# Making the first FFN column blocks' weight operands, and the sums of the values' weights, in other stages

## The chip, the cores and the metric

The kernel runs on one core of a Trainium2 chip (trn2). The metric is the device time of one execution in microseconds (us). The engines are TensorE (PE, its weight loads PEld), VectorE (DVE), ScalarE (ACT), GpSimd (POOL) and SyncE (SP). Each has a queue of its own that it works through in order; DMAs are issued from such a queue too.

## What is computed

Two layers on x of 1024 tokens by 1024 features, in float32. Layer 0 mixes the tokens with a chunked gMLP, layer 1 with differential attention, and each is followed by an FFN with a causal convolution of three taps. Each of the four parts stands between two RMSNorms and is added to its input:

```python
for layer in range(DEPTH):                       # 2
    y = rmsnorm(h, norm_g[layer, 0])
    y = gmlp_mixer(y, ...) if layer == 0 else diff_attention(y, ...)
    h = h + rmsnorm(y, norm_g[layer, 1])
    y = rmsnorm(h, norm_g[layer, 2])
    y = conv_ffn(y, w_up, conv_w, conv_b, w_down)   # 1024 -> 2 x 2816 -> 1024
    h = h + rmsnorm(y, norm_g[layer, 3])

def conv_ffn(x, w_up, conv_w, conv_b, w_down):
    h = causal_dwconv(x @ w_up, conv_w, conv_b)
    g, u = h[..., :D_FF], h[..., D_FF:]
    return (gelu(g) * u) @ w_down
```

## The kernel before

**Splits and passes.** Every float32 operand of a product is split (`split`, L170 and L173) in a hi part, which ScalarE casts to fp32r, and a lo part, the rest, which VectorE subtracts. A product takes three passes: hi by hi, hi by lo, lo by hi, all in `mm` (L162). Each 128x512 matmul of these is one instruction.

**Seven products for eight.** The FFN's up projection, its down projection and the values of the attention are computed as Strassen-Winograd products: the operands are cut in 2x2 blocks, sums of blocks are formed on both sides (S1 to S4 of the activations, T1 to T4 of the weights), and seven products take the place of eight. The sums of weights cost subtractions on POOL:

- the up projection forms them for each of its 22 column blocks in `winograd_weights` (L1044 and the lines behind it), from two raw loads of 512 KB, then splits seven parts;
- the down projection's sums are made beforehand by `weight_sum` (L438 to L447): two loads, four POOL subtractions of 128x256, two stores to DRAM (`td`). The values' weights `b_wv` go the same way into `tv`, in eight such sums: six in the loop of the mixer over the gate's column blocks g (at g = 4 to 7), two in layer 0's up projection (at j = 2 and 3). All loads and stores are issued from SP.

**The mixer** (`gmlp`) computes v in two halves, normalises it, mixes it with small matmuls in `gate` (L643 to L645: a copy on ScalarE, an addition on VectorE, an addition on POOL), and forms u in eight column blocks g (L693, L694, L677). At g = 4 `distances` makes the bias of the attention, 62 POOL operations (L596). Then the out projection begins, with operands `ops` split from the products.

**The FFN's opening** (`ffn`): column blocks 0 and 1 are begun together while the last rows of the normalised activations are still being turned (`xs`, L344, and transposes L334). Their weights are raw loads; their sums on POOL are partly pinned in program order (`early_sums`), their parts are split as they are needed.

**The down projection** (`down`) runs seven products of 11 blocks each, in the order A11·B11, A22·T4, A12·B21, A11·T2, A21·T1, A12·B22, A22·T3. Its operands are cast from `raw` into t8 tiles: one pair of blocks after the other, the last two pairs of a product ahead of the end, and for A22·T3 five pairs ahead, whose weights then lie in t8 tiles too. While A12·B22 and A22·T3 run, `end` normalises finished rows, and the transposes for the next stage follow.

**The values** (`values`) run the same kind of products behind layer 0's FFN, with T1 to T4 loaded from `tv` and S1 to S4 made by `finish`.

**What sets the order.** The program is traced in the order of the text, with `later` for work that is due after a number of matmul columns. A scheduler then orders each engine's instructions by when their inputs are expected; `keep_in_program_order` pins an instruction behind all that was traced before it on its engine. Tiles come from pools with a fixed number of buffers: t8 (8 KB of each partition, 15 buffers), wr (raw weights, 4), w4 (split weights, 7). A new tile waits until a buffer of its tag is free, and the buffers are handed out in program order.

Of the kernel before, what the change touches and what calls it, by code (L numbers as in the profile page):

```python
# [13 lines left out]
ALU = mybir.AluOpType  # L14
# [50 lines left out]
def trunk(ctx: ExitStack, tc: tile.TileContext, io):  # L65
# [202 lines left out]
    class WinogradOperand:  # L268
# [43 lines left out]
        def finish(self, tile=lambda: t8(F32R, (P, 4, 512))):  # L312
            for n in ("S2", "S1", "S4", "S3") if self.whole else ("S2", "S1", "S3", "S4"):
                hi, lo = self.part[n] = tile(), tile()
                for kt in range(4):
                    if self.whole and n == "S2":
                        self.sums((kt, slice(None)), nc.vector, nc.gpsimd)
                    split(hi[:, kt, :], lo[:, kt, :], self.raw[n][:, kt, :])
                yield
# [109 lines left out]
    def weight_sum(w, o, j):  # L429

        a = wpool.tile([P, 2, 2, 256], F32, tag="wr", name=nm("wr"), bufs=4)
        kt, cs = j // 2, slice(j % 2 * 256, j % 2 * 256 + 256)
        for k in range(2):
            src = w[kt + k * o.shape[1]].rearrange("p (b c) -> p b c", b=2)
            nc.sync.dma_start(a[:, k], src[:, :, cs])  # L438

        def rest():  # L440
            sub = nc.gpsimd.tensor_tensor
            sub(a[:, 0, 0], a[:, 0, 1], a[:, 0, 0], ALU.subtract)
            sub(a[:, 0, 1], a[:, 1, 1], a[:, 0, 1], ALU.subtract)
# [19 lines left out]
    def down(l, h_in, h_out, g_post, g_pre, y_next):  # L463
# [45 lines left out]
        def product(a, b, ahead=(), first=None, at=3, tail=SHORT_TAIL, wide=0):  # L509
# [11 lines left out]
            for m, (k, n) in enumerate(pairs[:-tail]):  # L521
                xw = ahead[m] if m < len(ahead) else operands(a, b, k, n)
                if m > 1 or b != "T4":
                    some(2)
                for i in range(4):
                    part(i, k, n, *xw)
                if m == at and first:
                    first()
            xws = [operands(a, b, k, n, m >= tail - wide) for m, (k, n) in enumerate(pairs[-tail:])]
# [10 lines left out]
        with tc.tile_pool(name=nm("out"), bufs=1) as pool:  # L540
# [40 lines left out]
    rd = dpool.tile([NT, P], F32, name="rd", tag="rd")  # L581

# [19 lines left out]
    def gmlp(y, y2, ahead):  # L602
        with tc.tile_pool(name="gm", bufs=1) as pool:
# [95 lines left out]
            for a in begun:  # L699
                a()  # L700
# [30 lines left out]
    def values(y):  # L731
# [7 lines left out]
        with tc.tile_pool(name="va", bufs=1) as pool:  # L739

            def product(a, b, groups=((0, 1), (2, 3))):
                ws = load(b)
# [25 lines left out]
            more = y.finish(lambda: pool.tile([P, 4, 512], F32R, tag="s", name=nm("s"), bufs=4))  # L768
            next(more)
            for t, r in product("A22", "T4"):  # L770
                nc.scalar.copy(v[:, t], r)
            next(more)
            for t, r in product("S2", "T2"):
                add(u2[:, t], r, u2[:, t], ALU.add)
                nc.gpsimd.tensor_tensor(v[:, t], v[:, t], u2[:, t], ALU.add)
            next(more)
            for t, r in product("S1", "T1"):
# [250 lines left out]

    def winograd_weights(pool, src, early):

        r1, r2 = raw_w(src[0], KT, P), raw_w(src[1], KT, P)
        b11, b21, b12, b22 = r1[:, 0:4, :], r1[:, 4:8, :], r2[:, 0:4, :], r2[:, 4:8, :]

        def part(b, pin=False):
            w = w4((2, 4, P))
            split(w[:, 0], w[:, 1], b, pin=pin)
# [7 lines left out]
        i = nc.gpsimd.tensor_tensor(t1, b12, b11, ALU.subtract)  # L1044
        if early:
            tc.keep_in_program_order(i)
        nc.gpsimd.tensor_tensor(t2, b22, t1, ALU.subtract)
        nc.gpsimd.tensor_tensor(t4, b21, t2, ALU.subtract)
        if early:
            yield  # L1050
            yield part(t4, True)
        nc.gpsimd.tensor_tensor(t3, b22, b12, ALU.subtract)
        for b in (t2, t1, t3, b22) if early else (t2, t1, t3, t4, b22):
            yield part(b)

    class Winograd:
# [47 lines left out]
        def early_sums(self):  # L1104
            next(self.weights)

# [35 lines left out]
    def ffn(l, y, h_in, h_out, g_pre, y2):  # L1142
        with tc.tile_pool(name=f"wg{l}", bufs=1) as wg, tc.tile_pool(name=f"ff{l}", bufs=1) as pool:
            def pair(j):
                return Winograd(wg, (io["ffn_up"][l, j], io["ffn_up"][l, NFF + j]), y, j < 2)
# [22 lines left out]
            for p in begun:  # L1168
                p.early_sums()
# [15 lines left out]
            for j in range(NFF):  # L1185
# [4 lines left out]
                if l == 0 and j in (2, 3):  # L1190
                    weight_sum(io["b_wv"], tv, KT - 4 + j)()
# [151 lines left out]
```

## Time and profile before

| | us |
|---|---|
| median of 3 runs | 2171.81 (2171.61 to 2175.49) |
| the profiled execution | 2170.53 |
| its span | 2168.8 |
| TensorE busy | 2113.0 (97%) |
| VectorE busy | 1660.5 (77%) |
| ScalarE busy | 1094.4 (50%) |
| POOL busy | 748.1 (34%) |

The profile is of one execution, whose own time stands beside the span. A timeline row gives the start, the duration (of several like instructions together, with their count behind x), the engine, the line, the operation, out<-in with shapes, and in brackets how long the engine was idle ahead of it and what ended that. The granted clock is the mean share of full speed at which TensorE ran in a stretch. The mean granted clock of the whole span is 0.995.

### The profile page before, as it was taken

The numbers are of one execution on the slowest core, as the hardware profiler recorded it, in microseconds if no ns is written. First come the engines' busy times: TensorE is split into PE (matmuls) and PEld (weight loads), VectorE is DVE, ScalarE is ACT, GpSimd is POOL, SyncE is SP. The second block draws the span as 40 slices with busy tenths as digits, with TensorE's granted clock in tenths as the row PEclk, the third lists the DMA queues.
The fourth block names the chain that finished last, engine by engine and source line by source line (L and its number), as shares of the span: only waits on it lengthen the run. The fifth ranks groups of instructions, "written<-read, shape, count | busy, mean of one in ns | idle before, by whom it ended". The sixth has DMA issues, their size and how long they took to land.

```text
span 2168.8 us, 27265 instructions
## 1 busy us (share of the span) xinstructions
PE 2113.0 (97%) x10008; PEld 1721.4 (79%) x10008; DVE 1660.5 (77%) x2031; ACT 1094.4 (50%) x1923; POOL 748.1 (34%) x691
## 2 busy tenths in 40 slices
PE   8989998999999999999999999999899999999998
PEld 7868776888888878887777777778688888888886
DVE  5755569878888786688588888866988888888756
ACT  7423435454545544465366665754555554454533
POOL 0463136666667000042001101222555666620012
PEclk9999999999999999999999999999999999999999
DMA  8332422544444562453411110233234444457324
GB/s 320 102 122 83 176 87 82 192 149 153 146 165 146 198 251 95 136 180 106 158 45 45 50 49 21 88 136 126 70 121 167 159 156 157 154 182 266 105 92 167
DMA packets 159270, 292.82 MB, mean 135 GB/s; under 512 B 12704, under 2 KB 77088, under 8 KB 159136
## 3 DMA queue, kind: packets, MB, share of 16 engines
q1 hardware_dynamic: 159136, 291.08, 39.3%
q8 instruction: 78, 1.28, 0.2%
q14 instruction: 56, 0.46, 0.1%
HBM read 214.49 MB, written 76.55 MB: 134 GB/s over the span
## 4 chain that ended last, share of the span: by engine, by line
PE 74%; DVE 9%; ACT 3%; issue 1%; POOL 0%; DMA 0%; DVEq 0%; ACTq 0%; POOLq 0%; SPq 0%
PE ps L162 70%; PE pst L162 2%; DVE t L173 2%; DVE w L173 1%; ACT e L885 1%; DVE t L1155 1%; PE pst L904 1%; PE pst L334 1%; DVE cols L1090 1%; DVE xs L344 0%; DVE e L891 0%; DVE h L385 0%; DVE sm L882 0%; DVE t L495 0%; ACT y L340 0%
## 5 line engine op out<-in xcount | busy, mean ns | idle before, releaser
L162 PE MATMUL ps<-t,w 128*128 128x512 f32 x4848 | 1150.8, 394 | 19.5 <-ACT tm L1086 7.8
L162 PEld LDWEIGHTS ps<-t,w 128*128 128x128 f32 x4848 | 899.2, 188 | 220.8 <-ACT tm L1086 11.6
L162 PE MATMUL ps<-w,t 128*128 128x512 f32 x2512 | 590.5, 392 | 9.0 <-ACT w L170 7.3
L162 PEld LDWEIGHTS ps<-w,t 128*128 128x128 f32 x2512 | 469.4, 188 | 107.1 <-ACT w L170 8.0
L173 DVE TENSOR_TENSOR w<-wr,w 128x512 fp32r<-128x512 f32 (+1 forms) x274 | 290.4, 1066 | 170.0 <-ACT w L170 84.3
L170 ACT CAST w<-wr 128x512 fp32r<-128x512 f32 (+1 forms) x276 | 219.1, 802 | 207.3 <-PE ps L162 195.2
L1155 DVE SCALAR_TENSOR_TENSOR t<-cols,cw,t 128x1023 f32<-128x1023 f32 (+1 forms) x176 | 264.1, 1500 | 18.9 <-ACT t L1153 16.8
L173 DVE TENSOR_TENSOR w<-wt,w 128x512 fp32r<-128x512 f32 x176 | 174.9, 1005 | 15.4 <-ACT w L170 15.2
L1086 ACT COPY tm<-ps 128x512 f32<-128x512 f32 x136 | 78.9, 580 | 146.7 <-PE ps L162 146.6
L173 DVE TENSOR_TENSOR t<-t,t 128x1024 fp32r<-128x1024 f32 (+1 forms) x124 | 134.0, 1109 | 14.4 <-ACT t L170 14.0
L170 ACT CAST t<-t 128x1024 fp32r<-128x1024 f32 (+1 forms) x124 | 105.7, 889 | 71.7 <-PE ps L162 59.4
L1153 ACT ACTIVATE t<-cols,cw 128x1024 f32<-128x1024 f32 x88 | 109.7, 1247 | 60.0 <-DVE cols L1090 59.8
L1044 POOL TENSOR_TENSOR wt<-wr,wr 128x512 f32<-128x512 f32 x44 | 67.3, 1529 | 195.5 <-DMA wr<-in_ffn_up 135.4
L162 PE MATMUL ps<-t,t 64*128 64x512 f32 (+4 forms) x792 | 128.3, 373 | 0.8 <-ACT e L885 0.4
L170 ACT CAST w<-wt 128x512 fp32r<-128x512 f32 x176 | 107.5, 622 | 23.2 <-PE ps L162 14.1
L559 POOL TENSOR_TENSOR v<-v,u 128x512 f32<-128x512 f32 x8 | 12.0, 1499 | 307.0 <-DVE u L558 307.0
L162 PEld LDWEIGHTS ps<-t,t 64*128 64x128 f32 (+1 forms) x792 | 90.3, 185 | 34.3 <-issue 11.0
L885 ACT ACTIVATE e<-ps,sm 128x128 f32<-128x128 f32 (+7 forms) x128 | 94.2, 744 | 28.8 <-DVE sm L877 22.7
L380 POOL TENSOR_SCALAR sm<-sm 128x1 f32<-128x1 f32 x32 | 22.3, 697 | 244.9 <-ACT y L378 244.6
L202 POOL TENSOR_SCALAR sm<-sm 128x1 f32<-128x1 f32 (+1 forms) x42 | 12.7, 303 | 263.7 <-ACT ot L924 161.2
L1090 DVE TENSOR_TENSOR cols<-ps,tm 128x512 f32<-128x512 f32 x132 | 90.1, 682 | 16.7 <-PE ps L162 15.0
L173 POOL TENSOR_TENSOR t<-wr,t 128x1024 fp32r<-128x1024 f32 (+1 forms) x16 | 36.4, 2282 | 167.9 <-ACT t L170 159.7
(156 smaller groups left out, 2480.4 us busy)
## 6 DMA issues: line engine op xcount, KB each, us to landing
wr<-in_ffn_up SPq DMA_DIRECT2D x88, 512.0 KB, 4.0
wr<-in_ffn_down SPq DMA_DIRECT2D x94, 256.0 KB, 3.7
pd<-t SPq DMA_DIRECT2D x88, 256.0 KB, 2.6
td<-wr SPq DMA_DIRECT2D x88, 256.0 KB, 2.5
wr<-td SPq DMA_DIRECT2D x40, 512.0 KB, 3.7
t<-pd SPq DMA_DIRECT2D x16, 1024.0 KB, 8.2
wr<-in_ffn_down SPq DMA_DIRECT2D x30, 512.0 KB, 3.6
hd<-h SPq DMA_DIRECT2D x24, 512.0 KB, 2.6
```

Source lines behind the costliest of these rows:

```text
L162: nc.tensor.matmul(o, a, b, start=first, stop=last, skip_group_check=onto)
L170: i = nc.scalar.copy(hi, src)
L173: return (engine or nc.vector).tensor_tensor(lo, src, hi.bitcast(F32), ALU.subtract)
L334: nc.tensor.transpose(pt[:, k * P:(k + 1) * P], xs[:, f:f + P], ident)
L380: nc.gpsimd.tensor_scalar(ss, sq[:, 0:1], sq[:, 1:2], EPS, ALU.add, ALU.add)
L885: nc.scalar.activation(e[:, :L], si[i], AF.Exp, bias=negm[:, i:i + 1], accum_out=sm[:, i:i + 1])
L904: nc.tensor.transpose(pt[:, k * P:(k + 1) * P], attn[:, c:c + P], ident)
L1044: i = nc.gpsimd.tensor_tensor(t1, b12, b11, ALU.subtract)
L1086: nc.scalar.copy(t, o)
L1090: nc.vector.tensor_tensor(o, a, b, ALU.add)
L1153: nc.scalar.activation(tt, src, AF.Identity, bias=c[:, 3:4], scale=c[:, 2:3])
L1155: nc.vector.scalar_tensor_tensor(tt[:, tap:], src[:, :S - tap], c[:, 2 - tap:3 - tap], tt[:, tap:], ALU.mult, ALU.add)
```

## The change

A new generator `presplit(l)` makes the split weight operands of the up projection's first two column blocks ahead of time and stores them to a DRAM buffer `ud[l]`. Each block takes two raw loads from SP into a t8 tile, four POOL subtractions, seven splits into t8 tiles and seven stores of 512 KB, issued from POOL's queue. `presplit(0)` is stepped through in the mixer's loop from g = 4 on, three steps at each half, and finished behind the loop; `presplit(1)` in layer 0's down projection, three steps behind each of the first four pairs of A12·B22 and the rest ahead of A22·T3.

The openings of both FFNs then load the seven parts of each block from `ud` into w4 buffers with SP, with no raw load, no sum and no split.

All eight sums of `b_wv` move into the product A21·T1 of layer 0's down projection, two behind each of its first four pairs. There they use a t8 tile in place of a wr tile, their first subtraction is pinned in program order, and their two stores are issued from POOL's queue.

In the values, T4, T2 and T1 are loaded and split ahead of the S parts that `finish` splits, and the casts of the S parts are pinned in program order.

```diff
-    def weight_sum(w, o, j):
+    def weight_sum(w, o, j, pin=False):
-        a = wpool.tile([P, 2, 2, 256], F32, tag="wr", name=nm("wr"), bufs=4)
+        if pin:
+            a = t8(F32, (P, 2, 2, 2, 256))[:, 0]
+        else:
+            a = wpool.tile([P, 2, 2, 256], F32, tag="wr", name=nm("wr"), bufs=4)
...
-            sub(a[:, 0, 0], a[:, 0, 1], a[:, 0, 0], ALU.subtract)
+            i = sub(a[:, 0, 0], a[:, 0, 1], a[:, 0, 0], ALU.subtract)
+            if pin:
+                tc.keep_in_program_order(i)
...
-                nc.sync.dma_start(o[k, kt][:, :, cs], a[:, k])
+                (nc.gpsimd if pin else nc.sync).dma_start(o[k, kt][:, :, cs], a[:, k])
...
+            beside = [lambda i=i: weight_sum(io["b_wv"], tv, i, True)() for i in range(KT if l == 0 else 0)]
             u4 = t8(F32, (P, 4, 512))
-            for i, r in product("A21", "T1"):
+            for i, r in product("A21", "T1", beside=[lambda n=n: (beside[2 * n](), beside[2 * n + 1]()) for n in range(len(beside) // 2)]):
...
-            for i, r in product("A12", "B22"):
+            early = presplit(1) if l == 0 else iter(())
+            def steps(n):
+                for _ in range(n):
+                    next(early, None)
+            for i, r in product("A12", "B22", beside=[lambda: steps(3)] * 4):
...
+            for _ in early:
+                pass
             for i, r in product("A22", "T3", tail=TAIL, wide=WIDE):
...
-            sums = {4: (0,), 5: (1, 2), 6: (3, 4), 7: (5,)}
-            begun = []
+            early = presplit(0)
             for g in range(8):
                 w = load_w(io["a_wu"][g], KT, P)
-                for a in begun:
-                    a()
-                begun = [weight_sum(io["b_wv"], tv, i) for i in sums.get(g, ())]
                 if g == 4:
                     distances()
                 for half in range(2):
+                    if g > 3:
+                        for _ in range(3):
+                            next(early, None)
...
+            t4 = load("T4")
             next(more)
-            for t, r in product("A22", "T4"):
+            for t, r in product("A22", "T4", ws=t4):
...
+    def presplit(l):
+        for p in range(2):
+            r = t8(F32)
+            for i in range(2):
+                nc.sync.dma_start(r[:, i, :].rearrange("p (k c) -> p k c", k=KT), io["ffn_up"][l, p + i * NFF])
+            b11, b21, b12, b22 = (r[:, i, h:h + 512].rearrange("p (k c) -> p k c", k=4) for i in (0, 1) for h in (0, 512))
+            yield
+            out = []
+            def put(n, b):
+                if not out:
+                    w = t8(F32R, (P, 2, 2, 4, P))
+                    out.extend((w[:, 0], w[:, 1]))
+                w = out.pop(0)
+                split(w[:, 0], w[:, 1], b)
+                nc.gpsimd.dma_start(ud[l][p, n], w.bitcast(F32))
+            for n, b in ((0, b11), (1, b21), (6, b22)):
+                put(n, b)
+                yield
+            for n, o, x, y in ((4, b11, b12, b11), (5, b12, b22, b12), (3, b22, b22, b11), (2, b21, b21, b22)):
+                nc.gpsimd.tensor_tensor(o, x, y, ALU.subtract)
+                yield
+                put(n, o)
...
     def winograd_weights(pool, src, early):
+        if early:
+            for n in range(7):
+                w = w4((2, 4, P))
+                nc.sync.dma_start(w.bitcast(F32), src[n])
+                yield w
+            return
...
-                if l == 0 and j in (2, 3):
-                    weight_sum(io["b_wv"], tv, KT - 4 + j)()
```

## Rows read from the trace of the kernel before

**Rows 1.** The page: the span, and the engines' busy times

```profile
span 2168.8 us, 27265 instructions
PE 2113.0 (97%) x10008; PEld 1721.4 (79%) x10008; DVE 1660.5 (77%) x2031; ACT 1094.4 (50%) x1923; POOL 748.1 (34%) x691
```

**Rows 2.** Busy time by stretch: span, PE, PEld, DVE, ACT, POOL, clock, DMA

```profile
122.00:160.00 38.00, 28.83 (x129) 23.50 (x128) 20.00 (x30) 10.44 (x19) 22.39 (x26) 0.87 0.41 132
...
171.00:215.00 44.00, 44.00 (x196) 36.44 (x196) 20.54 (x37) 12.71 (x18) 18.02 (x67) 1.00 0.19 62
```

**Rows 3.** Timeline of TensorE in the mixer: start, duration, line, operation, idle before

```profile
135.71 3.46 PE L162 MATMUL ps<-wsp,vp 128*128 128x128 f32 x15 [0.88 <-DVE vp L173]
140.97 13.20 PE L162 MATMUL ps<-t,w 128*128 128x512 f32 x48 [1.80 <-DVE t L644]
...
156.51 1.95 PE L162 MATMUL ps<-wsp,vp 128*128 128x128 f32 x15 [1.58 <-DVE vp L173]
```

**Rows 4.** Timeline of TensorE in layer 0's down projection

```profile
844.81 85.62 PE L162 MATMUL ps<-w,t 128*128 128x512 f32 x377
930.27 6.29 PE L162 MATMUL ps<-t,t 128*128 128x512 f32 x27
```

**Rows 5.** Timeline of POOL in the mixer

```profile
138.56 0.72 POOL L442 TENSOR_TENSOR wr<-wr 128x256 f32<-128x256 f32 x1 [5.51 <-DMA wr<-in_b_wv]
139.24 0.72 POOL L645 TENSOR_TENSOR t<-t,gt 128x256 f32<-128x256 f32 x1
```

**Rows 6.** Timeline of ScalarE in the mixer

```profile
139.99 0.37 ACT L643 COPY gt<-ps 128x256 f32<-128x256 f32 x1 [5.60 <-POOL t L645]
...
186.75 0.37 ACT L643 COPY gt<-ps 128x256 f32<-128x256 f32 x1 [12.52 <-POOL t L645]
```

**Rows 7.** Busy time by stretch, as rows 2, in the two openings

```profile
320.00:350.00 30.00, 23.78 (x100) 17.56 (x101) 29.09 (x37) 19.32 (x35) 19.32 (x12) 1.00 0.18 56
...
1528.00:1558.00 30.00, 23.71 (x100) 17.55 (x101) 29.09 (x35) 19.32 (x35) 18.85 (x12) 1.00 0.17 56
```

**Rows 8.** TensorE's waits from 310 to 375 us: total, times, longest

```profile
PE ps L162 <- ACT tm L1086: 3.9, 2, 2.1
PE ps L162 <- DVE w L173: 3.2, 3, 1.5
PE pst L334 <- DVE xs L344: 1.2, 1, 1.2
PE ps L162 <- ACT w L170: 0.9, 1, 0.9
```

**Rows 9.** The values: timelines of TensorE and VectorE, busy time by stretch

```profile
1005.99 4.39 PE L162 MATMUL ps<-w,s 128*128 128x512 f32 x12 [3.80 <-DVE w L173]
...
1004.72 3.48 DVE L173 TENSOR_TENSOR w<-wr,w 128x1024 fp32r<-128x1024 f32 x3
...
985.00:1050.00 65.00, 61.20 (x263) 49.94 (x262) 49.87 (x62) 21.21 (x32) 13.33 (x8) 0.97 0.34 115
```

**Rows 10.** VectorE's groups from 310 to 375 us: busy time, mean ns

```profile
L173 DVE TENSOR_TENSOR w<-wt,w 128x512 fp32r<-128x512 f32 x13 | 11.2, 876 | 0.0
L173 DVE TENSOR_TENSOR w<-wr,w 128x512 fp32r<-128x512 f32 x7 | 6.2, 914 | 0.0
```

**Rows 11.** Timelines of POOL and ScalarE in layer 0's down projection

```profile
867.10 2.14 POOL L559 TENSOR_TENSOR v<-v,u 128x512 f32<-128x512 f32 x1 [1.83 <-DVE u L558]
...
887.91 6.31 ACT L170 CAST t<-t 128x1024 fp32r<-128x1024 f32 x7
```

**Rows 12.** Instructions of two lines: shortest, median, longest ns, first and last start

```profile
L442 POOL TENSOR_TENSOR wr<-wr x52: 723/1182/1762, 102.0 to 1905.9; 128x256 f32<-128x256 f32 x52
...
L447 SPq DMA_DIRECT2D tv<-wr x16: 553/562/570, 104.5 to 375.2; - x16
```

**Rows 13.** Busy time by stretch, as rows 2, in layer 0's down projection

```profile
845.00:865.00 20.00, 20.00 (x90) 16.53 (x90) 12.49 (x13) 7.79 (x10) 3.59 (x3) 1.00 0.24 79
865.00:888.00 23.00, 23.00 (x103) 19.06 (x102) 7.46 (x7) 5.30 (x7) 2.40 (x2) 1.00 0.32 103
888.00:905.00 17.00, 17.00 (x77) 14.08 (x76) 14.62 (x16) 10.26 (x13) 0.00 (x0) 1.00 0.34 108
905.00:925.00 20.00, 20.00 (x90) 16.57 (x89) 16.68 (x18) 13.15 (x19) 3.22 (x4) 1.00 0.62 207
```

More of the change, by code (lines that the diff above doesn't have):

```diff
@@ L317, in finish @@
                         self.sums((kt, slice(None)), nc.vector, nc.gpsimd)
-                    split(hi[:, kt, :], lo[:, kt, :], self.raw[n][:, kt, :])
+                    split(hi[:, kt, :], lo[:, kt, :], self.raw[n][:, kt, :], pin=self.whole)
                 yield
@@ L507, in operands, with product @@
             return x, w
-        def product(a, b, ahead=(), first=None, at=3, tail=SHORT_TAIL, wide=0):
+        def product(a, b, ahead=(), first=None, at=3, tail=SHORT_TAIL, wide=0, beside=()):
             out = [bank1() for _ in range(4)]
@@ L528, in product @@
                     first()
+                if m < len(beside):
+                    beside[m]()
             xws = [operands(a, b, k, n, m >= tail - wide) for m, (k, n) in enumerate(pairs[-tail:])]
@@ L581, in trunk @@
     rd = dpool.tile([NT, P], F32, name="rd", tag="rd")
+    ud = [dpool.tile([2, 7, P, 2, 4, P], F32, name=f"ud{i}", tag=f"ud{i}") for i in range(2)]
     def distances():
@@ L698, in gmlp @@
                         weigh(g, half, u)
-            for a in begun:
-                a()
+            for _ in early:
+                pass
             flush()
@@ L739, in values, with product @@
         with tc.tile_pool(name="va", bufs=1) as pool:
-            def product(a, b, groups=((0, 1), (2, 3))):
-                ws = load(b)
+            def product(a, b, groups=((0, 1), (2, 3)), ws=None):
+                ws = ws or load(b)
                 os = [bank1() for _ in range(4)]
@@ L768, in values @@
             more = y.finish(lambda: pool.tile([P, 4, 512], F32R, tag="s", name=nm("s"), bufs=4))
+            t4 = load("T4")
             next(more)
-            for t, r in product("A22", "T4"):
+            for t, r in product("A22", "T4", ws=t4):
                 nc.scalar.copy(v[:, t], r)
+            t2 = load("T2")
             next(more)
-            for t, r in product("S2", "T2"):
+            for t, r in product("S2", "T2", ws=t2):
                 add(u2[:, t], r, u2[:, t], ALU.add)
                 nc.gpsimd.tensor_tensor(v[:, t], v[:, t], u2[:, t], ALU.add)
+            t1 = load("T1")
             next(more)
-            for t, r in product("S1", "T1"):
+            for t, r in product("S1", "T1", ws=t1):
                 add(u4[:, t], r, u2[:, t], ALU.add)
@@ L1027, in attention, with part @@
             return out
-    def winograd_weights(pool, src, early):
+    def presplit(l):
[20 more added lines that the diff above has]
+                put(n, o)
+    def winograd_weights(pool, src, early):
+        if early:
[4 more added lines that the diff above has]
+            return
         r1, r2 = raw_w(src[0], KT, P), raw_w(src[1], KT, P)
         b11, b21, b12, b22 = r1[:, 0:4, :], r1[:, 4:8, :], r2[:, 0:4, :], r2[:, 4:8, :]
-        def part(b, pin=False):
+        def part(b):
             w = w4((2, 4, P))
-            split(w[:, 0], w[:, 1], b, pin=pin)
+            split(w[:, 0], w[:, 1], b)
             return w
@@ L1043, in winograd_weights @@
         )
-        i = nc.gpsimd.tensor_tensor(t1, b12, b11, ALU.subtract)
-        if early:
-            tc.keep_in_program_order(i)
+        nc.gpsimd.tensor_tensor(t1, b12, b11, ALU.subtract)
         nc.gpsimd.tensor_tensor(t2, b22, t1, ALU.subtract)
         nc.gpsimd.tensor_tensor(t4, b21, t2, ALU.subtract)
-        if early:
-            yield
-            yield part(t4, True)
         nc.gpsimd.tensor_tensor(t3, b22, b12, ALU.subtract)
-        for b in (t2, t1, t3, b22) if early else (t2, t1, t3, t4, b22):
+        for b in (t2, t1, t3, t4, b22):
             yield part(b)
@@ L1102, in second @@
             self.add(self.cols[0][:, :512], self.product(self.first[1], "A12"), self.p1)
-        def early_sums(self):
-            next(self.weights)
         def early_part(self):
@@ L1144, in pair @@
             def pair(j):
-                return Winograd(wg, (io["ffn_up"][l, j], io["ffn_up"][l, NFF + j]), y, j < 2)
+                early = j < 2
+                src = [ud[l][j, n] for n in range(7)] if early else (io["ffn_up"][l, j], io["ffn_up"][l, NFF + j])
+                return Winograd(wg, src, y, early)
             def convolve(j, cols):
@@ L1167, in ffn @@
             begun = [pair(0), pair(1)]
-            for p in begun:
-                p.early_sums()
             cw = pool.tile([P, 2 * NFF, 4], F32, tag="cw", name="cw")
```

## The prediction

> **What bounds the kernel now.** The page's first section gives TensorE 2113.0 of 2168.8 us [rows 1]: nothing can be won beyond its 55.8 us of idle time and the few stretches in which its matmuls run slower. I therefore read the waits of TensorE first, then the busy times of the stretches that hold its gaps, then the timelines of the engines named there. The reader should see three places that the change touches, and one that it loads.
>
> *The mixer's end.* From 122 to 160 us TensorE is busy 28.83 of 38.00 us, so 9.2 us are gaps; the granted clock there is 0.87, about a quarter of the stretch at the lower of its two levels, 1.2 in place of 2.4 GHz [rows 2]. The gaps come ahead of small matmuls of the gate or right behind them, and the slower clock shows beside them: 15 matmuls of 128x128 take 3.46 us at 135.71 and 1.95 at 156.51, and 48 of 128x512 take 13.20 us at 140.97 [rows 3], where 48 times 0.227 us (377 in 85.62 us [rows 4]) are 10.9. That is 1.5 + 2.3, so 3.8 us of slowness; 13.0 us in all. The cause stands on POOL: the subtraction of a weight sum waited 5.51 us for its load, and the gate's addition L645 came only behind it [rows 5]; ScalarE waited 5.60 us for that addition before its copy L643 [rows 6], and the casts of the next tile stand behind that copy.
>
> *The two openings of the FFN.* From 320 to 350 us TensorE has 23.78 of 30.00, and 23.71 in the same stretch of layer 1, with VectorE at 29.09 of 30.00 in both [rows 7]. It waits for the lo parts of the weights, for the copies tm, and 1.2 us for xs [rows 8].
>
> *The values.* One gap of 3.80 us at 1005.99, for a lo part of T2 that VectorE began at 1004.72, behind splits of the S parts; the clock of 985 to 1050 is 0.97 [rows 9].
>
> *Layer 0's down projection*, where most of the new work goes, has no gap: 377 matmuls run from 844.81 to 930.43 without one [rows 4].
>
> **The change part by part.**
>
> *Weight sums out of the mixer.* Six of the eight leave POOL's queue in the mixer. With them goes the wait for its load [rows 5] and what follows from it. Bounds: 13.0 us if every gap and all the slow clock go, 4 if only the gaps right behind the 5.51 us wait do (0.88, 1.80 and the 1.5 of slowness at 135.71 [rows 3]). The waits are one cascade, so I take 11.
>
> *presplit(0) into the mixer.* Fourteen casts, 14 subtractions, 8 POOL subtractions, 4 loads and 14 stores, from the fifth of the eight column blocks on. There TensorE is full, 44.00 of 44.00, while VectorE has 20.54 and ScalarE 12.71 [rows 2]: 14 splits of 0.88 us on VectorE (the mean of w<-wt [rows 10]) are 12.3 us and fit. POOL is held by the distances, for which ScalarE waits 12.52 us without harm [rows 6]. The 15 buffers of tag t8 are almost all taken there, and the operands of the out projection queue for them behind presplit's tiles: 0 if presplit ends before 205 us, 6 if it ends at 215. I take 2.
>
> *The openings.* Of 20 weight splits on VectorE between 310 and 375 us [rows 10], 14 belong to the first two blocks and go; so do the 8 POOL subtractions beside them. Fourteen times 0.88 is 12.3 us of VectorE, more than the 6.2 us of gap in 320 to 350; VectorE would stand near 19 of 30. The gaps are 6.2 + 1.2 us in layer 0 and 6.3 + 1.2 in layer 1, 14.9 together; I leave 1 us in each for what is late next (the copies tm, or the first of the 512 KB loads that now wait for a w4 buffer), and take 13. The lower bound is 8: only the waits on w (3.2 and 0.9 a layer [rows 8]) go.
>
> *The values.* T4, T2 and T1 are split ahead of the S parts. VectorE's work is the same, only its order changes; the gap can go to the next S part. Bounds 0 and 5.2 (3.8, and 263 matmuls at 0.97 clock, some 1.4); I take 3.
>
> *What layer 0's down projection gets.* Eight weight sums in the product A21·T1 (32 POOL subtractions, 16 loads, 16 stores), presplit(1) in A12·B22 (8 POOL subtractions, 14 casts and splits, 14 stores). The first subtraction of each sum is pinned behind what POOL was given before, the last addition of v, which ends at 869.2 [rows 11]. A subtraction of this shape takes 0.72 to 1.76 us, median 1.18 [rows 12]; where VectorE is at 7.46 of 23 [rows 13] I take 0.8, later 1.2. No store has been issued from POOL in this trace. SP takes 0.56 us for one [rows 12], and this is the nearest row and my lower bound; the upper one is the longest of POOL's own instructions in the row beside it, 1.76. The value taken is 0.8, between the two and nearer to the row of a store. By that the sums end at 869.2 + 8 x (4 x 0.8 + 2 x 0.8) = 907.6. Behind them presplit(1)'s first block needs 4 subtractions and has 6 stores ahead of its last part: 4 x 1.2 + 6 x 0.8 = 9.6, so 917.2.
>
> Who waits: the operand tiles of A12·B22 and then of A22·T3 take their t8 buffers in program order behind presplit's, and their casts stand behind its casts on ScalarE; before, seven of them run in one burst at 887.91, far ahead of use [rows 11]. A22·T3's tail begins at 930.27 [rows 4], its first pair of 24 matmuls 5.45 us earlier, at 924.8; A12·B22 has 132 matmuls, 30.0 us, so it begins at 894.8 and needs its fourth pair at 911.2. That pair's cast (6.31 / 7 = 0.9 us [rows 11]) and split (3.48 / 3 = 1.2 [rows 9]) can follow the last presplit part's cast, 917.2 + 1.0 + 2.1: 920.3, so 9.1 us late. The second block ends one store, four subtractions and six stores later, 10.4 us; the operands of T3 come behind it with two casts and two splits a pair, while TensorE has been delayed by the 9.1 already, and I add 1 us. VectorE carries 14 more splits, 12.3 us, over 888 to 925, where it has 31.3 of 37 [rows 13]; what does not fit is within that delay. **Cost 10 us.** With 0.56 a store and 0.74 a subtraction: 869.2 + 36 x 0.74 + 22 x 0.56 + 3.1 = 911.2, no loss. With 1.18 and 1.76 it is 953.5, 42 us of loss.
>
> A rule of the Trainium skill speaks against this part: "SBUF — State Buffer", section "SBUF: two separate sides", says that a DMA issued from GpSimd's queue has its descriptors written by GpSimd, which VectorE can lock out of their common port during some of its operations. And "DMA: Bandwidth & Descriptors", section "SWDGE vs HWDGE vs iDMA", calls such DMAs slower to set up than those from SP; with some 1 us each, by an estimate from that page's figure of first-byte latency, the cost would be 14 us in place of 10. No row of before shows such a DMA.
>
> **The sum**, against the profiled run of 2170.5 us: 11 + 13 + 3 = 27 won, 10 + 2 = 12 lost, 15 net: 2155.5. The median of the runs lies 1.3 above the profiled one, so 2157.
>
> **The rivals.**
> *A: the cover holds.* Sums and presplit(1) end before 911 (stores as on SP, subtractions below 0.8). Then 27 less 2 is won: 2147 (2142 to 2150). For it: POOL has 3.59 us of work in 845 to 865 and none in 888 to 905 [rows 13]. Against it: the pin at 869.2.
> *B: the gaps are filled, not emptied.* The mixer's gates then wait behind presplit(0)'s stores as they did behind the sums, and the openings wait for tm and for loads instead of w: half of 11 and 8 in place of 13, less 2 and the 5 us of a milder backlog: 16.5 - 7 = 9.5 at best, 5 with the backlog of 10: 2162 to 2167.
> *C: the backlog takes all.* A loss of 21 to 29 us in the down projection, which stores of 1.1 to 1.5 us give with subtractions of 1.0 (872.3 + 36 + 22 x 1.3 = 936.9, 26 late): no change, 2168 to 2176.
> *D: slower.* The same mechanism at one place, the pair of A12·B22 needed at 911.2, with dearer stores: at 1.76 and 1.18 us 42 are lost, 17 more than the 25 won: 2189. It decides from 1.5 us a store on at 1.0 a subtraction (1.2 at 1.18), where the loss passes 29. For it: nothing on POOL runs in parallel, and 30 stores stand in its queue. Against it: it needs the upper half of a price that no row tells.
>
> **How the numbers follow.** The forecast (2150 to 2161) 0.42, A 0.18, B 0.12, C 0.14, D 0.14. A difference under 0.2%, 4.3 us, is about what a measurement of this kernel cannot tell from no change. Faster by more: the forecast, A and B, 0.72; within: C, 0.14; slower: D, 0.14. Range 2142 to 2180: it leaves out less than a tenth on either side, D's far end and a gain over what the gaps allow.
>
> **What would show it.** In the mixer: POOL's waits for in_b_wv gone, TensorE near 37 of 38 us in 122 to 160, the clock at 1.00. In the openings: TensorE over 28 of 30 us, no wait on w. In the values: no gap over 1 us. In the down projection: a gap of some 9 us ahead of A12·B22's fourth pair or at A22·T3's beginning, with POOL busy without a break from 869 to 925. If that gap is absent, the price of a store or the order of the tiles was read wrongly and A holds. If POOL's stores each hold it for over 1.5 us, D does. The prediction is also wrong if the out projection's first operands come after 215 us.

## The result and the profile after

The changed kernel takes 2196.9 us (median of 4 runs, 2196.33 to 2197.77) against 2173.65 of before in the same comparison: a ratio of 1.0106, 95% interval 1.0091 to 1.0121, so 23 us slower. The forecast was 2157 us, range 2142 to 2180. The two profiled executions, which the differences below compare, lie 26.3 us apart (2196.82 and 2170.53).

Both traces hold 10008 matmuls. Subtracting the start of the n-th in one from that in the other gives the difference stage by stage (negative: the change is ahead):

| matmul no., place (us in before) | change minus before, us |
|---|---|
| 650, late in the gates (161) | -15.3 |
| 1375, layer 0's opening begins (320) | +6.4 |
| 1600, opening done (382) | -3.2 |
| 3700, near the end of A11·T2 (860) | -3.3 |
| 4300, down projection done (991) | +38.2 |
| 4400, values (1019) | +32.7 |
| 7200, layer 1's opening begins (1513) | +32.7 |
| 7500, opening done (1591) | +25.4 |
| 10007, last | +26.3 |

So all four gains are there: 15.3 in the mixer, 9.6 and 7.3 from the openings' first matmuls on, 5.5 in the values. Two losses outweigh them: 21.7 us between the gates and the opening, 41.5 in the down projection.

The page's first lines of the changed kernel (as [rows 1]), and TensorE's waits in the whole run (total, times, longest):

```profile
span 2195.0 us, 27447 instructions
PE 2117.2 (96%) x10008; PEld 1726.1 (79%) x10008; DVE 1661.9 (76%) x2031; ACT 1094.5 (50%) x1923; POOL 768.5 (35%) x735
...
PE ps L162 <- ACT t L170: 24.6, 4, 14.2
PE pst L334 <- DVE xs L344: 13.4, 6, 3.7
PE ps L162 <- DVE t L173: 8.2, 6, 4.4
PE pst L334 <- ACT t L294: 6.7, 4, 4.1
PE ps L162 <- ACT w L170: 6.4, 1, 6.4
...
PE ps L162 <- DVE w L173: 1.8, 1, 1.8
```

VectorE's busy time is the same to 1.4 us; work was moved, not added. The waits on w fell from 21.1 us to 8.2, and 6.4 of these stand at the kernel's first matmul, as before; those on t (operands in t8 tiles) have come in.

Busy time by stretch, columns as [rows 2], in the mixer, the opening and the down projection (answers to [rows 2, 7, 13]):

```profile
122.00:160.00 38.00, 38.00 (x197) 32.49 (x196) 18.54 (x32) 12.15 (x24) 22.99 (x65) 1.00 0.25 84
...
200.00:215.00 15.00, 1.87 (x9) 1.21 (x7) 12.22 (x19) 6.12 (x10) 5.05 (x6) 0.71 0.35 140
...
320.00:350.00 30.00, 26.34 (x114) 21.58 (x114) 19.22 (x29) 15.38 (x28) 5.80 (x7) 0.94 0.41 136
...
326.40:356.40 30.00, 30.00 (x131) 24.89 (x130) 23.89 (x34) 19.00 (x32) 3.87 (x3) 0.95 0.28 91
...
865.00:888.00 23.00, 15.99 (x65) 12.49 (x64) 7.44 (x5) 3.67 (x4) 20.66 (x26) 0.87 0.67 208
...
984.00:1010.00 26.00, 16.42 (x70) 12.85 (x70) 21.54 (x25) 17.34 (x33) 5.41 (x10) 0.74 0.47 167
```

The stretch of 122 to 160 is full, at full clock. From 320 to 350 the opening holds a wait for xs (below); over the like matmuls, 6.4 us later, TensorE has all 30.00 us and VectorE 23.89, more than the forecast 19. From 865 to 888 TensorE works 15.99 of 23 us while VectorE (7.44) and ScalarE (3.67) mostly idle and POOL is busy (20.66): none of the three lacks time, and what they wait for is POOL's work.

*The gap ahead of the out projection*, timelines of TensorE, ScalarE, POOL, SP:

```profile
163.24 38.63 PE L162 MATMUL ps<-t,w 128*128 128x512 f32 x168 [1.84 <-DVE u L710]
216.07 0.79 PE L162 MATMUL ps<-w,t 128*128 128x512 f32 x1 [14.20 <-ACT t L170]
...
172.23 0.62 ACT L170 CAST t<-t 128x512 fp32r<-128x512 f32 x1 [10.41 <-DMA t<-in_ffn_up]
...
149.88 14.40 POOL L614 TENSOR_TENSOR t<-t 128x36 f32<-128x36 f32 x58
...
197.17 5.86 POOL L1072 TENSOR_TENSOR t<-t 128x512 f32<-128x512 f32 x4
...
155.27 9.39 SPq L617 DMA_DIRECT2D bd<-t  x2
164.71 0.51 SPq L1054 DMA_DIRECT2D t<-in_ffn_up  x1
```

TensorE finished u's products at 201.9, 13 us earlier than before, and found no operand. ScalarE stood 10.41 us at a presplit cast whose raw load came late: SP issued it at 164.71, behind the stores of distances (`bd`), whose last operation on POOL ended at 164.3. Behind that cast stood the activations of u. The out projection's first matmul came at 216.07, so the sign that the prediction had set for this place, after 215 us, is there.

*The down projection*, timelines of TensorE, ScalarE, POOL (one sum in full), and the line that issues the sums' stores; then the first sum's loads and its first subtraction:

```profile
849.69 28.50 PE L162 MATMUL ps<-w,t 128*128 128x512 f32 x125
884.16 0.80 PE L162 MATMUL ps<-w,t 128*128 128x512 f32 x1 [5.97 <-ACT t L170]
...
883.07 1.04 ACT L170 CAST t<-t 128x1024 fp32r<-128x1024 f32 x1 [14.66 <-DMA tv<-t]
...
906.02 2.61 ACT L170 CAST t<-t 128x512 fp32r<-128x512 f32 x4 [10.71 <-POOL t L445]
...
872.65 0.85 POOL L445 TENSOR_TENSOR t<-t 128x256 f32<-128x256 f32 x1
873.58 0.74 POOL L448 TENSOR_TENSOR t<-t 128x256 f32<-128x256 f32 x1
874.40 0.74 POOL L449 TENSOR_TENSOR t<-t 128x256 f32<-128x256 f32 x1
875.08 0.67 POOL L452 DMA_DIRECT2D tv<-t  x1
875.70 0.83 POOL L450 TENSOR_TENSOR t<-t 128x256 f32<-128x256 f32 x1
876.97 0.69 POOL L452 DMA_DIRECT2D tv<-t  x1 [0.45 <-POOL t L450]
...
908.87 0.69 POOL L452 DMA_DIRECT2D tv<-t  x1 [0.41 <-POOL t L450]
...
L452 POOL DMA_DIRECT2D tv<-t x16: 672/682/749, 870.1 to 908.9; - x16
...
  ACT t L170: 24.1, 4
...
842.86 1.25 SPq L441 DMA_DIRECT2D t<-in_b_wv  x2
...
865.92 1.72 POOL L445 TENSOR_TENSOR t<-t 128x256 f32<-128x256 f32 x1
```

The sum shown takes POOL 5.0 us, and the eight stand one behind the other from 865.92 to 909.6. The line `ACT t L170` says who waited for their stores: ScalarE's casts of operand tiles, 24.1 us in four waits, the first until 883 in A21·T1 itself. The first sum's loads had landed by 847.2, yet its first subtraction, pinned behind the last addition of v, came 18.7 us later; all that time it held its tile.

*The openings' beginning*, POOL's timeline, in before and in the change:

```profile
316.77 0.19 POOL L202 TENSOR_SCALAR sm<-sm 128x1 f32<-128x1 f32 x1 [2.35 <-ACT y L340]
...
317.56 1.29 POOL L1044 TENSOR_TENSOR wt<-wr,wr 128x512 f32<-128x512 f32 x1
...
315.14 1.30 POOL L1097 TENSOR_TENSOR wt<-wr,wr 128x512 f32<-128x512 f32 x1
...
323.85 0.19 POOL L202 TENSOR_SCALAR sm<-sm 128x1 f32<-128x1 f32 x1
```

In before, the first block's pinned subtraction came behind the rsqrt L202 of the last row block. With the first two blocks' subtractions gone, those of the third, which have no pin, run ahead of it. TensorE waited for the xs behind it 3.65 us in either layer (until 326.14 and 1563.26), where before it waited 1.2 ([rows 8]).

### The profile page after: what moved, and what is told of

Its sections match the earlier page's. It is cut to its first block, busy times and chain, and to the rows that moved or that the text cites. A ratio compares the mean times of both kernels' runs of the same rounds, so it can differ in the third digit from the quotient of the medians.

```text
span 2195.0 us, 27447 instructions
## 1 busy us (share of the span) xinstructions
PE 2117.2 (96%) x10008; PEld 1726.1 (79%) x10008; DVE 1661.9 (76%) x2031; ACT 1094.5 (50%) x1923; POOL 768.5 (35%) x735
## 5 line engine op out<-in xcount | busy, mean ns | idle before, releaser
L162 PE MATMUL ps<-w,t 128*128 128x512 f32 x2512 | 601.0, 397 | 39.6 <-ACT t L170 24.6
L162 PEld LDWEIGHTS ps<-w,t 128*128 128x128 f32 x2512 | 476.1, 191 | 143.6 <-ACT t L170 26.3
L173 DVE TENSOR_TENSOR w<-wr,w 128x512 fp32r<-128x512 f32 (+1 forms) x262 | 284.5, 1090 | 167.6 <-ACT w L170 88.4
L170 ACT CAST w<-wr 128x512 fp32r<-128x512 f32 (+1 forms) x264 | 212.6, 811 | 201.0 <-PE ps L162 189.2
L173 DVE TENSOR_TENSOR t<-t,t 128x1024 fp32r<-128x1024 f32 (+1 forms) x152 | 154.8, 1050 | 66.5 <-ACT t L170 65.2
L170 ACT CAST t<-t 128x1024 fp32r<-128x1024 f32 (+1 forms) x152 | 122.0, 839 | 153.8 <-PE ps L162 62.8
L173 DVE TENSOR_TENSOR w<-wt,w 128x512 fp32r<-128x512 f32 x160 | 159.5, 1006 | 14.6 <-ACT w L170 14.6
L170 ACT CAST w<-wt 128x512 fp32r<-128x512 f32 x160 | 98.7, 623 | 19.9 <-PE ps L162 16.5
L202 POOL TENSOR_SCALAR sm<-sm 128x1 f32<-128x1 f32 (+1 forms) x42 | 11.3, 270 | 253.2 <-ACT ot L944 161.2
L162 PE MATMUL ps<-wx,t 128*128 128x512 f32 x384 | 90.6, 391 | 0.5 <-ACT wx L170 0.4
```

Of the source, the lines that this page charges most:

```text
L162: nc.tensor.matmul(o, a, b, start=first, stop=last, skip_group_check=onto)
L170: i = nc.scalar.copy(hi, src)
L173: return (engine or nc.vector).tensor_tensor(lo, src, hi.bitcast(F32), ALU.subtract)
L202: nc.gpsimd.tensor_scalar(ss, ss, 1.0 / n, EPS, ALU.mult, ALU.add)
```

## The experiments

The table gives the same differences as above (kernel minus before at eight matmuls), from each run's trace, always against the one trace of before; the last column is the time of that one execution beside one of before in the same comparison.

| run | 650 | 1375 | 1600 | 3700 | 4300 | 4400 | 7200 | 7500 | us; before |
|---|---|---|---|---|---|---|---|---|---|
| sums_only | -14.3 | -14.5 | -14.4 | -14.9 | +8.4 | +9.5 | +8.5 | +8.6 | 2180.1; 2170.9 |
| sums_in_up | -14.6 | -14.3 | -14.2 | +28.8 | +28.8 | +29.7 | +28.9 | +28.9 | 2199.8; 2170.9 |
| pre0 | -14.2 | +8.4 | +1.7 | +37.2 | +37.2 | +37.4 | +37.0 | +37.0 | 2209.2; 2170.9 |
| pre1 | -15.1 | -14.8 | -12.8 | +23.8 | +46.1 | +40.6 | +40.9 | +35.1 | 2207.1; 2170.9 |
| sums_ring | -15.1 | -15.2 | -15.1 | -15.2 | +10.2 | +11.5 | +13.8 | +13.8 | 2186.0; 2170.1 |
| sums_nosub | -15.0 | -15.1 | -15.0 | -16.0 | -16.0 | -15.8 | -16.3 | -16.4 | 2155.1; 2170.1 |
| values_only | -0.2 | 0.0 | 0.0 | -0.2 | -0.2 | -3.2 | -4.2 | -4.2 | 2166.6; 2170.1 |
| v2 | -14.9 | +17.7 | +8.1 | +7.6 | +7.6 | +6.1 | +28.2 | +22.5 | 2193.6; 2170.1 |
| sums_dve | -15.2 | -15.3 | -15.2 | -15.9 | -11.1 | -12.5 | -13.3 | -13.3 | 2158.8; 2173.9 |
| change_dve | -14.9 | +1.1 | -7.9 | -8.6 | +8.2 | +2.7 | +2.9 | -2.8 | 2168.3; 2173.9 |
| v2_dve | -14.0 | +0.9 | -8.4 | -7.7 | -7.8 | -10.8 | -0.6 | -5.2 | 2166.0; 2173.9 |
| mix1 | -15.3 | -9.4 | -15.1 | -15.3 | -0.2 | -5.6 | -3.9 | -11.5 | 2160.5; 2170.5 |
| mix0 | -15.0 | -7.2 | -14.6 | -15.4 | -8.5 | -11.5 | -11.2 | -11.3 | 2160.3; 2170.5 |
| mix2 | -14.0 | -6.8 | -14.2 | -14.0 | -6.9 | -10.0 | -10.9 | -10.9 | timed below |

A second execution of the kernel of sums_dve gave -13.9 at 3700 and -7.7 at 4300, so one kernel's columns can differ by 3.4 us from execution to execution, and the loss of a stage by 1.4.

**The sums alone.** sums_only is before with the diff's `weight_sum`, its call in A21·T1 and nothing else of the change.

> Only the eight weight sums are moved into A21·T1, as the change has them; nothing is presplit and the values are as before. Theory (order of the t8 buffers): the mixer wins 15 us up to its out projection and has no gap there; in the down projection the operand tiles of A21·T1 wait for buffers that the sums hold, first gap near the end of A21·T1, 9 to 14 us lost; in all 2 to 6 us faster than before. Rival (the splits of presplit are the load, the sums are hidden): nothing lost there, 15 us faster.

It lost 23.3 us in the down projection and ends 9 slower. The sums pay for more than half of the loss by themselves; the theory had the place right and the size too small.

sums_nosub leaves out the 32 subtractions, and with them the pin of the first of each sum:

```diff
-            sub(a[:, 0, 0], a[:, 0, 1], a[:, 0, 0], ALU.subtract)
...
+            if not pin:
+                sub(a[:, 0, 0], a[:, 0, 1], a[:, 0, 0], ALU.subtract)
```

> As sums_only, without the 32 subtractions of the sums on POOL (the raw weights are stored, so the values are computed from wrong sums); loads, tiles, stores and the values' products stay. Theory: the line of buffers moves on as fast as loads and stores land, so the loss of 23 us falls to under 8; the pace of POOL is what makes the line long. Rival (the line and the traffic hurt by themselves): over 15 us stay.

Nothing was lost: TensorE's row has no gap where sums_only (second row) had 5.5 us and more.

```profile
839.68 74.74 PE L162 MATMUL ps<-w,t 128*128 128x512 f32 x329
...
872.12 0.80 PE L162 MATMUL ps<-w,t 128*128 128x512 f32 x1 [5.54 <-ACT t L170]
```

Tiles in line, loads and 16 stores from POOL cost nothing by themselves. The 32 subtractions, 0.8 us each, and their pins together cost 23 us; the first store of a sum left POOL at 833.5 here and at 858.5 in sums_only.

sums_ring, the line shortened to two tiles:

```diff
-            a = t8(F32, (P, 2, 2, 2, 256))[:, 0]
+            if j == 0:
+                ring[:] = [t8(F32, (P, 2, 2, 2, 256)) for _ in range(2)]
+            a = ring[j // 2 % 2][:, j % 2]
```

> As sums_only (which lost 23 us in the down projection), but the eight sums share two t8 tiles, granted once at the beginning of A21·T1, in place of eight half-used ones in line between the operand tiles. Loads, POOL's work and stores are the same. Theory (the operand tiles stand in line for buffers behind the sums): at most 6 of the 23 us stay. Rival (the added POOL work, loads and stores are the load, or SP's waiting loads hold the weights back): 15 us or more of the loss stays.

The theory failed here: A21·T1 lost nothing, but a single gap of 14.7 us followed in A12·B22, and 25.4 us went in all.

```profile
905.45 26.76 PE L162 MATMUL ps<-w,t 128*128 128x512 f32 x108 [14.72 <-ACT w L170]
...
893.22 1.99 ACT L170 CAST t<-t 128x1024 fp32r<-128x1024 f32 x2 [17.58 <-POOL t L452]
```

ScalarE stood 17.58 us at one cast, with the casts of w that TensorE needed behind it. By the addresses in the compiled program, that tile had been given the buffer of the ring that POOL gave back at 891.1, though another buffer was free from 871.7 on. Which buffer a tile gets is fixed when the program is built. So it is not the number of tiles in line. The likeliest reading, which no run tests, is that the plan expects POOL to be done sooner than it is: somebody is handed the late buffer, and an in-order queue passes the wait on.

sums_dve, the same sums on VectorE (and the new order of the values):

```diff
-            sub = nc.gpsimd.tensor_tensor
+            sub = (nc.vector if pin else nc.gpsimd).tensor_tensor
```

> Sums in A21·T1 as in sums_only, with their 32 subtractions on VectorE in place of POOL, and the new order of the values; nothing is presplit. Theory (POOL's pace, 5 us a sum in one line, is what the operand tiles wait for; VectorE stands at 7.5 of 23 us there and takes some 0.4 us for such a subtraction): the down projection loses under 5 of the 23 us, and with 15 won in the mixer and 4 in the values the run is 14 to 19 us faster than before. Rival (tiles in line hurt whoever does the sums): 15 us or more lost, not faster than before by over 4.

4.8 us lost in place of 23.3. A subtraction takes 0.42 us there, half of POOL's 0.83, and the first comes at 842.11, 12 us sooner than POOL's in sums_only (third row), because on VectorE the pin does not hold it behind v's additions on POOL. Which of the two counts more was not separated: a run with the subtractions on POOL and no pin is missing.

```profile
L450 DVE TENSOR_TENSOR t<-t x8: 409/416/426, 846.1 to 875.1; 128x256 f32<-128x256 f32 x8
...
842.11 0.42 DVE L445 TENSOR_TENSOR t<-t 128x256 f32<-128x256 f32 x1
...
854.31 1.72 POOL L445 TENSOR_TENSOR t<-t 128x256 f32<-128x256 f32 x1
```

sums_dve_t is the same kernel, executed four times:

> The kernel of sums_dve, timed: only the sums moved, on VectorE, and the new order of the values. Theory: 12 to 16 us faster than before, ratio 0.9925 to 0.9945, so the gain of moving the sums stands outside the spread of the runs. Rival (the single look was a lucky execution): ratio above 0.996.

2158.63 us against 2172.69: 0.9933 (0.9916 to 0.9949), 14 us faster than before and 38 faster than the change; the down projection of its trace lost 6.2 us.

**The sums in the up projection** (sums_in_up): one more `weight_sum` at j = 2 to 9 of `ffn(0)`.

> The eight sums leave the mixer for layer 0's up projection, one in each of the column blocks 2 to 9, with wr tiles and stores from SP as the two of before; nothing else is changed. Theory: the mixer's 15 us are won and nothing is lost anywhere: 13 to 15 us faster than before. Rival (the up projection has no room for loads, POOL and stores): under 8 us.

A miss: 43 us lost there. TensorE waits for tm, up to 9.2 us at once. ScalarE, whose copies these are, waits 88.8 us for POOL's sums of the up projection's own weights (0.9 in before), which stand among the moved ones, and 28.4 us for raw weights, most likely because the moved sums hold wr buffers that the next column block's 512 KB loads need.

```profile
498.38 21.92 PE L162 MATMUL ps<-t,w 128*128 128x512 f32 x84 [9.18 <-ACT tm L1133]
...
ACT w L170 <- POOL wt L1099: 56.4, 14, 5.8
ACT w L170 <- POOL wt L1094: 32.4, 9, 4.9
ACT w L170 <- DMA wr<-in_ffn_up: 28.4, 10, 10.0
```

pre0 and pre1 stand on this kernel, so they are read by their stages alone.

> As sums_in_up, and layer 0's first two blocks are presplit in the mixer as in the change; layer 1 and the values as before. Theory (the presplit work stands in the queues of VectorE, ScalarE and POOL ahead of the last column blocks' u): the 15 us won up to 201 us are lost in one gap of 14 us ahead of the out projection, the opening gives 6 to 9: 3 to 9 us faster than before. Rival (that gap came from the moved sums): 21 to 24 us faster.

presplit(0) loses 22.6 us between 650 and 1375 with the sums gone from the down projection: the gap is its own.

> As sums_in_up, and layer 1's first two blocks are presplit in layer 0's down projection as in the change; layer 0's opening and the values as before. Theory: without the sums' backlog POOL is free at 889, so A21·T1 loses nothing, but the presplit tiles still stand ahead of the operand tiles of A12·B22 and A22·T3: 5 to 15 us lost there, 6 won in layer 1's opening: 6 to 16 us faster than before. Rival 1 (only the backlog of the sums hurts): nothing lost, 21 us faster. Rival 2 (the extra splits are the load): all of the change's 30 us behind A21·T1 are lost, 9 us slower than before.

presplit(1) loses 22.3 us between 3700 and 4300 without any backlog of sums, more than the theory's 15 and less than rival 2's 30. So the losses nearly add: 23.3 for the sums alone and 22.3 for presplit(1) alone, against 41.5 for both.

**Other places.** v2 puts the sums and presplit(0) into the mixer's out projection, presplit(1) into the attention's:

```diff
+        def beside(t):
+            for a in begun:
+                a()
+            begun[:] = [weight_sum(io["b_wv"], tv, t, pool_stores=True)]
+            for _ in range((5, 5, 6)[t] if t < 3 else 99):
+                next(early, None)
```

> The change with its work in other places: all eight sums in the mixer's out projection (one for each row block, wr tiles, stores from POOL), presplit(0) there too (from its first three row blocks), presplit(1) in the attention's out projection; nothing of it in the down projection; the values in the new order. Theory (where the t8 line and POOL are free the same work costs nothing): 15 us won in the mixer, no gap ahead of the out projection, 6 to 8 in each opening, 3 to 5 in the values: 24 to 34 us faster than before. Rival (the work costs wherever it stands): under 10 us.

32.6 and 22.1 us lost up to the two openings, in the out projections: xs waits there for POOL's rsqrt, which stands among the sums' and presplit's subtractions. The rival held. v2_dve has their subtractions on VectorE:

> As v2 (all the work in the out projections), which lost 30 us in layer 0's out projection and 25 in layer 1's because xs waited for POOL's rsqrt behind sums and presplit's subtractions; here the subtractions are on VectorE. Theory: the waits for xs go, 15 + 15 + 4 us are won and under 10 lost: 20 to 32 us faster than before. Rival (the presplit's casts and loads in the queues of ScalarE and VectorE hold end's work back by themselves): 15 us or more lost in each out projection, within 10 us of before.

14.9 and 10.2 us are still lost, more than the openings give, so the theory failed here; what holds those rows was not traced further. change_dve is the change with all subtractions on VectorE, at the diff's places:

> The whole change, with the subtractions of the sums and of both presplits on VectorE; stores stay on POOL's queue. Theory: of the 41 us lost in the down projection under 15 stay, and of the 14 us gap ahead of the out projection under 7: 10 to 30 us faster than before. Rival (VectorE, which has some 17 us free between 888 and 965, becomes the bound by the 27 us more that it gets): 25 us or more lost in the down projection, no faster than before.

Of 41.5 us 16.8 stay, of the 21.7 ahead of the opening 16.0, and the run is 5.7 us faster; the theory wanted less than 15 and 7 to stay and 10 won. So the subtractions on POOL, with their pins there, account for more than half of the first loss and for little of the second.

**What holds the out projection.** mix1 is change_dve with `distances()` behind presplit(0) and the third block's first subtraction pinned; mix0 leaves presplit(1) out; mix2 calls `distances()` behind the out projection's operands, its stores from POOL.

> As change_dve, with two edits: distances (62 operations on POOL, two t8 tiles) is called behind presplit(0) in place of ahead of it, and the third column block's first POOL subtraction is pinned in program order in both FFNs. Theory: of the 12 us that change_dve still lost ahead of the out projection most go, since presplit's first casts waited 10.9 us for distances' store and 8.3 us for a load behind it in SP's queue; the waits for xs at the openings' beginning (3.7 and 3.2 us, POOL's rsqrt behind the third block's subtractions) go too: mixer and opening 20 to 24 us ahead of before at 376 us, in all 18 to 28 us faster. Rival (the presplit's own splits delay u and the weighing): 8 us or more still lost ahead of the out projection, under 12 us faster in all.

> As mix1 without presplit(1): layer 1's opening as before, and in the down projection only the sums, on VectorE. Theory: the down projection loses 4 us as in sums_dve, not 16; layer 1's opening wins nothing. Ahead of mix1 by 2 to 6 us, if presplit(1) costs more there (8 to 12) than the opening gives back (6 to 9); the rival says that with VectorE doing the subtractions presplit(1) pays, and mix1 is ahead by 2 to 6.

```profile
155.99 43.77 PE L162 MATMUL ps<-t,w 128*128 128x512 f32 x192
199.59 4.92 PE L162 MATMUL ps<-w,t 128*128 128x512 f32 x21
210.80 8.70 PE L162 MATMUL ps<-w,t 128*128 128x512 f32 x25 [6.29 <-DVE w L173]
...
204.91 2.00 ACT L170 CAST t<-t 128x1024 fp32r<-128x1024 f32 x2 [6.69 <-DMA bd<-t]
```

In mix0 192 matmuls run without a gap beside presplit(0), whose last store leaves POOL at 177.6: with its subtractions on VectorE it costs nothing once distances is not ahead of it. Of what is lost now (7.8 us to no. 1375), 6.29 us are one gap behind distances, whose store `bd<-t` an operand tile waits for. The pin worked: the wait for xs at the openings is back at 0.2 us where it was set (1.2 in mix0's layer 1, which is as before). But the theory's 18 us and more did not come: mix1 is 10 us faster. mix1 and mix0 take the same time: presplit(1) costs 8.2 us more in the down projection (15.1 against 6.9) and gives 7.6 back in the opening.

> As mix0, with distances called behind the out projection's operand tiles and its two stores issued from POOL's queue. Theory: in mix0 the mixer's matmuls ran without a gap beside presplit(0), and the 8 us lost behind them came with distances' tiles and their stores in SP's queue, ahead of the out projection's operands and weights; out of that line they go: 20 us or more ahead of before at 376 us, 13 to 18 us faster in all (ratio 0.992 to 0.994). Rival (the loss is the presplit's and comes back in another place, or POOL's 14 us of distances now hold the first rsqrt of end): at most 15 us ahead at 376 us, no faster than mix0.

2161.0 us, 0.9943 (0.9928 to 0.9957), no better than mix0: POOL began distances at 210.7, held the first rsqrt until 230.8, and TensorE waited 5.87 us for xs. The rival held.

```profile
210.69 11.77 POOL L614 TENSOR_TENSOR t<-t 128x660 f32<-128x660 f32 x32 [32.28 <-DMA t<-in_rel_bias]
...
230.80 0.30 POOL L380 TENSOR_SCALAR sm<-sm 128x1 f32<-128x1 f32 x1
...
236.54 1.97 PE L334 MATMUL pst<-ident,xs 128*128 128x128 f32 x8 [5.87 <-DVE xs L344]
```

**The values alone.**

> The kernel before with nothing but the new order of the loads and splits in the values. Theory: the gap of 3.8 us ahead of S2·T2 goes and no other takes its place, 3 to 5 us faster. Rival (in pre1, with the old order, the values' stretch shrank by 5 us after a delay upstream, so the order may give nothing by itself): within 1 us of before.

3.5 us faster in its one execution, 4 by the trace.

```profile
1004.59 37.47 PE L162 MATMUL ps<-w,s 128*128 128x512 f32 x164 [1.73 <-DVE s L173]
```

The gap of 3.80 us is gone. One of 1.73 for an S part has come in, and the clock of 985 to 1050 is 1.00 in place of 0.97. But pre1, with the old order, gains 5.5 us in the values too (46.1 to 40.6) after its delay upstream; so the 5.5 of the change, which comes behind such a delay, can't be put down to the order.

## Why the prediction was wrong

**What was right.** *The mixer:* 11 us were taken, 15.3 came, 0.9 of it in the first 20 us, where the kernels do the same; the cascade from the wait for in_b_wv was read rightly, and even the upper bound of 13.0 was low. *The openings:* 13 taken, 14.1 came: 9.6 less the 2.8 that the wait for xs took just ahead of no. 1375, and 7.3, from which the like 2.4 in layer 1 are off already. I had named the copies tm and the loads as what is late next; it was xs, and its cause, a pin that the diff removes, I had listed nowhere. *The values:* 3 taken, 4 for the order alone; the change has 5.5, but see pre1. *POOL's prices:* 0.8 a store and a subtraction were taken, the sums' end forecast for 907.6; stores took 0.68 and 0.54, subtractions 0.72 to 0.85 in 25 of 32 cases and up to 1.72 in the others, and the sums ended at 909.6. That the two ends agree is in part luck: the sums began 3.3 us earlier than taken, at 865.9, and lasted 43.6 us in place of 38.4. So the rival that the outcome resembles, D, fell by its own condition: its stores were to cost over 1.5 us.

**The step that failed** is "Who waits" in the down projection, 10 us taken and 41.5 measured. I let the first late operand be the fourth pair of A12·B22, behind presplit(1)'s last part, needed at 911.2. The first was the fourth pair of A21·T1, needed at 881.3 in before, some 30 us earlier, and late behind the tiles of the sums: it began at 884.16, after a wait of 5.97 us. I had counted POOL's work up to its end and compared that with the last need; but each sum holds a buffer from its load to its store, and the next operand tiles are handed exactly those buffers. sums_nosub, without the subtractions and their pins, loses nothing; sums_dve, where they start sooner and take half as long, loses 4.8. How much of it is the pin and how much POOL's pace stays open.

The delay also did not stop at one gap, where I had added 1 us. By the starts of single matmuls the 41.5 us come in five steps: 9.6 at the fourth pair of A21·T1 (no. 3792), 7.8 at the second pair of A12·B22 (3876), 6.9 from its fifth pair on (3948), 3.9 in A22·T3 up to no. 4160, and 13.3 behind that, among the last rows' transposes. sums_only has 8.5 at the first step and nothing behind no. 4160; pre1, without sums there, has 6.4 at the third and 12.3 behind no. 4160. So the sums made the first step and presplit(1) the last: the work of `end` moved back, and from 984 to 1010 TensorE had little beside the last rows' transposes, 16.42 of 26 us at a granted clock of 0.74, part of it at 1.2 in place of 2.4 GHz.

**The second** is presplit(0) in the mixer, 2 us taken, 21.7 measured between gates and opening (14.2 of it one gap, about 3 the wait for xs). I wrote that distances hold POOL "without harm", from a trace in which nothing but the gates stood behind them. With presplit behind them, its tiles and loads waited for distances, and u for its casts. The margin I had looked at was busy time (VectorE 20.54 of 44); the time that counted was that of the first wait. mix0 shows that the work itself fits, with the subtractions on VectorE.

**The range** ended at 2180 because I set the loss's upper end aside as a price that is too dear, when my own formula gave 42 us at that end. That 42 stands beside the measured 41.5 is luck: it is worked out for one gap, at prices of a store and a subtraction that did not come.

## What to carry to other kernels

Before work is moved onto an idle engine, ask how long each piece holds its buffer and who is handed that buffer next; an engine that was idle for 90% of a stretch (POOL from 865 to 888, 2.40 of 23 us busy [rows 13]) is slow all the same when eight pieces of 5 us stand in one line. A gap on the main engine can be won in one place and lost in another by nothing but the order of queues, so weigh a change stage by stage, by the same instruction's start in both traces. When a diff moves work, look for the pins and orders that it drops on the way.

## What the hardware showed

A store issued from POOL's queue held POOL 0.54 us (ud's, 512 KB, 28 of them) or 0.68 us (tv's, 256 KB, 16 of them), where SP's issue of a store of tv took 0.56 us ([rows 12]), and its stores landed a little later than SP's of the same sizes: ud's of 512 KB after 4.1 us (SP's stores of hd 2.7), tv's of 256 KB after 3.3 (SP's, in before, 2.5). The prediction's second price, some 1 us by an estimate from the first-byte latency in the Trainium skill's "DMA: Bandwidth & Descriptors" (section "Specifications"), was too high for what a store holds POOL here. The starving that the Trainium skill's "SBUF — State Buffer" (section "SBUF: two separate sides") describes is not to be seen in these issues: none took over 0.78 us, also from 935 to 955, where VectorE was busy 18.74 of 20 us and three stores at 941.76 took 1.63 together. But VectorE ran no plain copy in this trace, the operation that the Trainium skill's page names for it, so that case is not tested.

One subtraction of a sum took POOL 0.72 to 0.85 us in most cases and 1.07 to 1.72 in seven of 32. Each of the seven ran beside a split on VectorE; that split can be longer too, as the one at 887.53, which took 1.95 us where others of its shape took 1.21.
